# Seven-product 1024-column panels and ScalarE convolution taps in the channel mixers of a two-layer decoder trunk

## The chip, the cores and the metric

The kernel runs on one core of one Trainium2 chip. The metric is device time in microseconds (us) from the first to the last instruction of the program with what lies around it, as the median of several executions. The engines of the core have their own instruction queues: TensorE (PE, matmuls), with its weight loads shown apart as PEld; VectorE (DVE); ScalarE (ACT); GpSimd (POOL); SyncE (SP), which issues most of the DMAs. Matmul results land in PSUM, which has eight banks of 128 x 512 fp32.

## The reference, cut to what matters

There are 256 tokens, a model width of 2048 and two layers. Layer 0 mixes tokens by gated linear attention and layer 1 by forgetting attention; both also attend into 256 memory tokens. After each mixer comes a channel mixer, which is what the change touches:

```python
def causal_dwconv(u, w, b):
    up = jnp.pad(u, ((0, 0), (CONV_WIDTH - 1, 0), (0, 0)))
    return w[0] * up[:, 0:s_] + w[1] * up[:, 1:s_ + 1] + w[2] * up[:, 2:s_ + 2] + b

def conv_ffn(h, w_up, conv_w, conv_b, w_down):
    u = causal_dwconv(h @ w_up, conv_w, conv_b)
    a, val = split_cols(u, [FFN_HIDDEN, FFN_HIDDEN])
    return (jax.nn.silu(a) * val) @ w_down
```

The hidden width is 5632 (44 chunks of 128), so `w_up` is 2048 x 11264 and `w_down` is 5632 x 2048. Input to the mixer is `h = rmsnorm(x, norm_ffn)`, and its output is added to `x`. Everything is fp32.

## The kernel before

**Split products.** TensorE runs in the type fp32r. To keep fp32 accuracy each operand is held as a high part and a low part (the rest), and a product of two operands is three matmuls: high by high, low by high, high by low. The activations are the stationary operand (128 channels x 128 tokens); the weights are the moving operand (128 channels x up to 512 columns). There are two token blocks b of 128 tokens.

**Weight units.** Weights stream from HBM in units of 128 x 1024 fp32 (512 KB, tile `raw`, four buffers). ACT casts a unit to its high part `whi` (L207) and DVE subtracts that to get the low part `wlo` (L208), four buffers each. These instructions carry a priority of 300 places ahead of where they stand, so the planner puts them first as soon as a buffer is free. The planner (Tile's scheduler) lists the instructions of each engine in a fixed order by priority and by its own simulated times; the order on PE can therefore differ from that of the source.

**Panels.** An ordinary panel (`panel_tm`, matmuls at L310; `proj_tm`, matmuls at L282) has 512 output columns for both token blocks in two PSUM banks, and eight units of two channel chunks each: 8 x 2 x 2 x 3 = 96 matmuls for 16 chunks. The banks come from two pools: `acc` (four banks, tag acc) and the work banks (`ps_s` two, `ps_o` one, `ps_t` one).

**The channel mixer** (`ffn`, L1285) goes over the 44 hidden chunks in three parts (`PARTS`: 16, 16 and 12 chunks). In each part, up panels of two hidden chunks (256 columns of each half) come first. When an up panel is done, DVE transposes its two blocks out of PSUM by 32 x 32 squares (L611), a DMA writes them to DRAM (`far`) and four DMAs bring them back with channels on partitions (`close`). Then `convolve` works on one pair of hidden chunks: for each of the four 128 x 256 pieces DVE multiplies by the norm's row (L1306), ACT makes the last tap with scale and bias (L1310), DVE adds the other two taps (L1311, L1312); then ACT does silu (L1314), DVE multiplies the halves (L1315), and the result is split into high (L465) and low (L466) parts in the chunk buffers `m`. After the part's up panels the down panels of that part add to `x`. The first units of the down panels run while the last chunks of `m` are still being made.

**Pairs with seven products.** In parts 0 and 1, output columns 0 to 1023 are two ordinary panels, run nearly side by side. Output columns 1024 to 2047 are one panel over eight banks (`pair_tm`, L338): a chunk takes 12 matmuls (L377), but two chosen pairs of chunks (`SEVEN`) are handled as a 2 x 2 block product with seven products in place of eight (Winograd's form of Strassen's scheme): 21 matmuls (L363) in place of 24. For that DVE makes four sums of weight blocks (L393 to L396), which are split as well (L325, L326), and four sums of activations per pair (L1322 to L1325), and at the end combines p1, p5, p6 and p7 (L406 to L409). In part 2 all four down panels are ordinary.

**The norm.** The mixer's norm factor per token is applied after the up product, in `convolve`, as a row over tokens (`nx.row`), which costs a small matmul pair (L545).

## Time and profile before

| what | value |
|---|---|
| median of 3 runs | 2232.63 us (2232.56 to 2235.64) |
| the profiled execution, time | 2233.26 us |
| its span, first to last instruction | 2231.5 us |
| mean granted TensorE clock | 0.999 |
| PE busy | 2220.2 us (99%), 10405 matmuls |
| PEld busy | 1869.1 us (84%) |
| DVE busy | 1647.4 us (74%) |
| ACT busy | 1200.5 us (54%) |
| DMA queue of the weights | 510.66 MB, 73.2% of 16 engines |

The busy share of an engine says how full it is over the whole span, and the groups by line say what fills it. A mean of one instruction's duration is longer than the distance from its start to that of the next, when several follow each other without a gap; that distance, called pitch below, is read from a stretch of equal instructions in the timeline or in the chain. PE's durations overlap in this way above all. The chain of work that ended last tells which engine set the end at each moment.

### The profile page before, as it was taken

How to read it: one execution, taken by the hardware profiler on the slowest of the kernel's cores; microseconds unless marked ns; L12 is line 12 of the kernel's file. 1: busy time of each engine (PE TensorE's matmuls, PEld its weight loads, DVE VectorE, ACT ScalarE, POOL GpSimd, SP SyncE). 2: the span in 40 equal slices, each digit the busy share in tenths (PEclk: the TensorE clock that was granted, in tenths of full speed). 3: DMA queues.
4: the chain of work that ended last, by engine and by line, in shares of the span. 5: the costliest groups of instructions: out<-in, count | busy, mean ns of one | idle time of the engine just before them, and what ended most of it. 6: DMA issues, size and time to landing. Idle time of an engine off the chain costs nothing.

```text
span 2231.5 us, 29658 instructions
## 1 busy us (share of the span) xinstructions
PE 2220.2 (99%) x10405; PEld 1869.1 (84%) x10405; DVE 1647.4 (74%) x2754; ACT 1200.5 (54%) x1779; POOL 3.4 (0%) x19
## 2 busy tenths in 40 slices
PE   9999999999999999999999999999999999999998
PEld 7888888888888888888888998888888888888886
DVE  7768977668777687866777569666877677775776
ACT  6655664555554455545565455454655455553554
POOL 0000000000000000000000000000000000000000
PEclk9999999999999999999999999999999999999999
DMA  9777667777776777667787767778786678766774
GB/s 348 231 222 223 194 187 244 250 234 247 246 223 205 227 241 244 204 213 237 240 244 251 214 195 244 226 244 258 242 242 201 217 237 242 242 200 217 240 245 142
DMA packets 183053, 513.34 MB, mean 230 GB/s; under 512 B 20588, under 2 KB 66296, under 8 KB 182776
## 3 DMA queue, kind: packets, MB, share of 16 engines
q1 hardware_dynamic: 182328, 510.66, 73.2%
q8 instruction: 81, 1.33, 0.2%
q10 hardware_dynamic: 576, 0.79, 0.1%
q14 instruction: 68, 0.56, 0.1%
HBM read 468.63 MB, written 42.74 MB: 229 GB/s over the span
## 4 chain that ended last, share of the span: by engine, by line
PE 98%; DMA 1%; DVE 1%; ACT 0%; SPq 0%; issue 0%; DVEq 0%
PE acc L310 71%; PE ps_s L310 9%; PE acc L282 5%; PE ps_s L377 3%; PE acc L238 3%; PE ps_o L377 1%; PE ps_t L377 1%; PE acc L236 1%; PE acc L363 1%; PE ps_s L363 0%; PE ps_s L959 0%; DMA fky<-far 0%; DMA raw<-wp 0%; PE ps_o L635 0%; PE ps_s L635 0%; PE ps_o L363 0%
## 5 line engine op out<-in xcount | busy, mean ns | idle before, releaser
L208 DVE TENSOR_TENSOR wlo<-raw,whi 128x1024 fp32r<-128x1024 f32 (+4 forms) x793 | 948.2, 1198 | 502.5 <-ACT whi L207 483.4
L207 ACT ACTIVATE whi<-raw 128x1024 fp32r<-128x1024 f32 (+4 forms) x793 | 825.1, 1042 | 781.7 <-PE acc L310 504.2
L310 PE MATMUL acc<-whi,B 128*128 128x512 f32 (+3 forms) x2672 | 647.7, 380 | 0.0
L310 PEld LDWEIGHTS acc<-whi,B 128*128 128x128 f32 x2672 | 494.4, 188 | 83.5
L310 PE MATMUL acc<-whi,mix 128*128 128x512 f32 x1488 | 369.0, 389 | 0.0
L310 PE MATMUL acc<-wlo,B 128*128 128x512 f32 (+3 forms) x1336 | 352.7, 380 | 0.0
L310 PEld LDWEIGHTS acc<-whi,mix 128*128 128x128 f32 x1488 | 279.2, 188 | 57.9
L310 PEld LDWEIGHTS acc<-wlo,B 128*128 128x128 f32 x1336 | 248.2, 188 | 42.3
L310 PE MATMUL acc<-wlo,mix 128*128 128x512 f32 x744 | 200.4, 390 | 0.0
L310 PEld LDWEIGHTS acc<-wlo,mix 128*128 128x128 f32 x744 | 139.6, 188 | 28.9
L310 PE MATMUL acc<-whi,A 128*128 128x512 f32 x592 | 150.4, 389 | 0.0
L310 PEld LDWEIGHTS acc<-whi,A 128*128 128x128 f32 x592 | 111.1, 188 | 23.1
L1310 ACT ACTIVATE cv<-u,cw 128x256 f32<-128x256 f32 x176 | 95.1, 592 | 55.6 <-DVE u L1306 54.8
L310 PE MATMUL ps_s<-whi,mix 128*128 128x512 f32 x336 | 83.8, 389 | 0.0
L310 PE MATMUL acc<-wlo,A 128*128 128x512 f32 x296 | 83.6, 389 | 0.0
L1312 DVE SCALAR_TENSOR_TENSOR cv<-u,cw,cv 128x256 f32<-128x256 f32 x176 | 77.6, 478 | 0.0
L1311 DVE SCALAR_TENSOR_TENSOR cv<-u,cw,cv 128x256 f32<-128x256 f32 x176 | 76.0, 472 | 0.0
L310 PEld LDWEIGHTS ps_s<-whi,mix 128*128 128x128 f32 x336 | 63.0, 188 | 13.0
L310 PEld LDWEIGHTS acc<-wlo,A 128*128 128x128 f32 x296 | 55.4, 188 | 11.4
L1314 ACT ACTIVATE cv<-cv 128x256 f32<-128x256 f32 x88 | 36.7, 418 | 35.3 <-DVE cv L1312 31.7
L310 PE MATMUL ps_s<-whi,B 128*128 128x512 f32 x208 | 52.5, 389 | 0.0
L238 PE MATMUL acc<-mix,whi 128*128 128x512 f32 x192 | 48.9, 394 | 0.0
(346 smaller groups left out, 2062.8 us busy)
## 6 DMA issues: line engine op xcount, KB each, us to landing
raw<-wp SPq DMA_DIRECT2D x743, 512.0 KB, 4.3
fvt<-far SPq DMA_DIRECT2D x100, 128.0 KB, 5.8
raw<-wp SPq DMA_DIRECT2D x32, 384.0 KB, 3.4
yzu<-far SPq DMA_DIRECT2D x96, 128.0 KB, 5.7
far<-yu SPq DMA_DIRECT2D x22, 512.0 KB, 2.8
far<-yzu SPq DMA_DIRECT2D x22, 512.0 KB, 2.9
raw<-wp SPq DMA_DIRECT2D x24, 388.0 KB, 3.7
far<-blk SPq DMA_DIRECT2D x12, 512.0 KB, 3.4
```

The costliest lines, as they stand in the source:

```text
L207: casts.append(S.activation(hi[:, s], raw[:, s], AF.Copy))
L208: lows.append(V.tensor_tensor(lo[:, s], raw[:, s], hi[:, s].bitcast(F32), ALU.subtract))
L236: mm = TE.matmul(acc[p][c][:, :T], w[:, s], both[:, 0, :], start=False, stop=end and j == 3)
L238: mm = TE.matmul(acc[p][c], w[:, s], both, start=u == j == 0, stop=end and j == 3)
L282: mm = TE.matmul(acc[b][:, :n], src[kcs[j] - base][:, part, b * P : (b + 1) * P], w, start=u == 0 and low == part == j == 0, stop=u == end ...
L310: mm = TE.matmul(acc[b][:, :n], src[kc - base][:, part, b * P : (b + 1) * P], ready[low][:, j * n : (j + 1) * n], start=i == low == part = ...
L363: r = TE.matmul(bank[name], x[a], w[b], start=name not in begun, stop=last and i == 2)
L377: r = TE.matmul(bank[name], tok(k, b)[part], w[low][:, h * 512 : (h + 1) * 512], start=name not in begun, stop=last and low == 1)
L1310: S.activation(r, u[:, 2:], AF.Identity, bias=w[3], scale=w[2])
L1311: V.scalar_tensor_tensor(r, u[:, 1 : T + 1], w[1], r, ALU.mult, ALU.add)
L1312: V.scalar_tensor_tensor(r, u[:, :T], w[0], r, ALU.mult, ALU.add)
L1314: S.activation(cv[0], cv[0], AF.Silu)
```

## The change

It edits the channel mixers of both layers and what they use.

- Up panels: 20 of the 22 per layer are joined two by two into panels of 1024 columns (`WIDE`, ten per layer), which run through `pair_tm` with 16 units of one channel chunk each. One pair of input chunks (4 and 5, `SEVEN_UP`) goes by seven products in each; the sums of the inputs for it (`input_sums`) are made once per layer. Two ordinary up panels remain in part 2.
- Down panels: in parts 0 and 1 both halves of the output columns are now panels of 1024 columns with two pairs by seven products (`SEVEN_DOWN`, chunks 4 and 8 of the part); they run one after the other. In part 2 columns 0 to 1023 are one panel of 1024 columns without such pairs, and the two last panels stay ordinary.
- Banks: `pair_tm` uses four banks that live over the whole panel (p2, p3, p4, x) and four that live only from the first to the last seven-product pair (p1, p5, p7, p6). `flip` swaps from panel to panel which four come from `acc` and which from the work banks. `early` combines p1, p5, p6, p7 right behind the last such pair, `late` adds p2, p3, p4, x at the end. The weights of a pair are loaded into a tag of their own, `raw2`, with two buffers, and summed in place.
- The norm factor is applied per token block as a column (`nx.col`, a scale per partition) when an up panel is read from PSUM, so `nx.row` goes, and the transposes read SBUF instead of PSUM.
- `convolve`: for each piece ACT writes all three taps (one with scale and bias, two with a scale), 12 ACT instructions per call; DVE adds them in two instructions over 1024 elements; silu and the product of the halves are one instruction each over 512 elements.
- `close` is called at other places: at units 7 and 11 of the next up panel, at units 7 and 9 of the first down panel of parts 0 and 1, and at unit 4 of that of part 2.
- Room in SBUF: scratch tiles of the norms move to the pool of the stage, the final gain is loaded late into the input buffers, and the last panel's last three weight units are split by 512 columns into those buffers (`split_apart`).

```diff
--- before.py
+++ after.py
+WIDE = ((0, 4, 8, 12), (16, 20, 24, 28), (32, 36))
+SEVEN_UP = (4,)
+SEVEN_DOWN = (4, 8)
...
-                tm(("up", l, j), ("ffn_w_up", l), j * P, 2 * P, more=[(HID + j * P, 2 * P)])
+                if j in WIDE[p]:
+                    cols = [(c + (j + i) * P, 2 * P) for i in (0, 2) for c in (0, HID)]
+                    out.append((("up", l, j), ("ffn_w_up", l), full, cols, 1))
+                elif j - 2 not in WIDE[p]:
+                    tm(("up", l, j), ("ffn_w_up", l), j * P, 2 * P, more=[(HID + j * P, 2 * P)])
             last = p == len(PARTS) - 1
+            for f in (0, 2):
+                if f and last:
+                    break
+                out.append((("down", l, p, f), ("ffn_w_down", l), list(range(lo, hi)), [(f * 512, 1024)], 1))
+            for f in (2, 3) if last else ():
...
+        fast, slow = ("p1", "p5", "p7", "p6"), ("p2", "p3", "p4", "x")
+        accs, works = (slow, fast) if flip else (fast, slow)
+        tags = {n: ("acc", 4) for n in accs}
+        tags.update(zip(works, (("o", 1), ("s", 2), ("s", 2), ("t", 1))))
...
+            plan.append(k)
+            k += 2 if k in sums else 1
...
+        for k in plan:
+            if k in sums:
+                with tc.high_priority(offset=AHEAD):
+                    ra, rb = [pool.tile([P, NUNIT], F32, name="raw2", tag="raw2", bufs=2) for _ in range(2)]
+                    for t, (off, _, w) in ((ra, units[k]), (rb, units[k + 1])):
+                        loads.append(nc.sync.dma_start(t, wp[off : off + P * w].rearrange("(p n) -> p n", p=P)))
+                st = [[sums[k][:, part, j, :] for part in range(2)] for j in (3, 0, 1, 2)]
+                done = k == end[-1]
+                w1 = split_more(ra[:, :512], 512)
+                w2 = split_more(rb, 1024)
+                with tc.high_priority(offset=AHEAD):
+                    V.tensor_tensor(ra[:, :512], ra[:, 512:], ra[:, :512], ALU.subtract)
+                    V.tensor_tensor(ra[:, 512:], rb[:, 512:], ra[:, 512:], ALU.subtract)
+                    V.tensor_tensor(rb[:, 512:], rb[:, 512:], ra[:, :512], ALU.subtract)
+                    V.tensor_tensor(rb[:, :512], rb[:, :512], rb[:, 512:], ALU.subtract)
+                three("p1", tok(k, 0), [t[:, :512] for t in w1], done)
+                three("p2", tok(k + 1, 0), [t[:, :512] for t in w2])
+                three("p3", st[3], [t[:, 512:] for t in w2])
+                w3 = split_more(ra, 1024)
+                three("p5", st[0], [t[:, :512] for t in w3], done)
+                three("p7", st[2], [t[:, 512:] for t in w3], done)
+                w4 = split_more(rb, 1024)
+                three("p6", st[1], [t[:, 512:] for t in w4], done)
+                last_mm.append(three("p4", tok(k + 1, 1), [t[:, :512] for t in w4]))
+                if done:
+                    early(bank)
+                hooks.get(k + 1, int)()
+            else:
                 w = split_unit(units[k])
                 last = k == n - 1
+                steps = [(low, *place) for low in range(2) for place in places]
...
+                for low, name, b, h in steps:
+                    for part in range(2 - low):
+                        r = mm(name, tok(k, b)[part], w[low][:, h * 512 : (h + 1) * 512], last and low == 1)
+                    if last and low:
+                        ends.append(r)
+                        late(b, h, bank[name])
                 last_mm.append(r)
+            hooks.get(k, int)()
+    def token_sums(r, dst):
+        t = r.rearrange("p s (b n) -> p (s b) n", b=2)
+        a11, a21, a12, a22 = (t[:, n, :] for n in range(4))
+        V.tensor_tensor(a22, a21, a22, ALU.add)
+        V.tensor_tensor(a21, a11, a21, ALU.subtract)
+        V.tensor_tensor(a11, a22, a11, ALU.subtract)
+        V.tensor_tensor(a12, a12, a11, ALU.subtract)
+        halves([dst[:, part] for part in range(2)], t)
...
+    def down_pair(l, p, f, src, sums, flip, pool, temps, then=None, hooks={}):
+        def early(bank):
+            t0, t1 = temps()
+            S.activation(t0, bank["p1"], AF.Copy)
+            add_to(f)(0, t0)
+            V.tensor_tensor(t0, bank["p6"], t0, ALU.add)
+            V.tensor_tensor(t1, bank["p7"], t0, ALU.add)
+            add_to(f)(1, t1)
+            add_to(f + 1)(1, t1)
+            add_to(f + 1)(1, bank["p5"])
+            V.tensor_tensor(t0, bank["p5"], t0, ALU.add)
+            add_to(f + 1)(0, t0)
+        def late(b, h, a):
+            add_to(f + h)(b, a)
+            if then is not None:
+                then(f + h, b)
+        pair_tm(where["down", l, p, f], src, sums, flip, pool, early, late, hooks)
...
                         col = (c * 44 + j + s) * 4
                         w = [cw[:, col + n : col + n + 1] for n in range(4)]
+                        src = z[:, :, 2 * c + s]
+                        S.activation(by_run(taps[0][:, s, c, :]), src, AF.Identity, bias=w[3], scale=w[2])
+                        S.activation(by_run(taps[1][:, s, c, 1:]), src, AF.Copy, scale=w[1])
+                        S.activation(by_run(taps[2][:, s, c, 2:]), src, AF.Copy, scale=w[0])
+                t = taps[0]
+                for i_ in (1, 2):
+                    V.tensor_tensor(t, t, taps[i_][:, :, :, :T], ALU.add)
+                S.activation(t[:, :, 0, :], t[:, :, 0, :], AF.Silu)
+                r = fp.tile([P, 2, T], F32, name="cv", tag="cv")
+                V.tensor_tensor(r, t[:, :, 0, :], t[:, :, 1, :], ALU.mult)
+                for s in range(2):
+                    split(m, i + s, r[:, s, :])
...
+            def input_sums(k):
+                r = fp.tile([P, 2, T], F32, name="cv", tag="cv")
+                for s in range(2):
+                    V.tensor_tensor(r[:, s, :], h[k + s][:, 0, :].bitcast(F32), h[k + s][:, 1, :].bitcast(F32), ALU.add)
+                up_sums[k] = held("usum", k)
+                token_sums(r, up_sums[k])
...
+            def turn(j, i):
 
                 count[0] += 1
-                return panel_tm(("up", l, j), h, done, second)
+                y = ys[count[0] % 2]
+                def evac(b, a):
+                    with tc.high_priority(offset=AHEAD):
+                        V.transpose(y[:, :, :, b, :], a.rearrange("p (k c i) -> p c k i", c=4, i=32))
+                    if b:
+                        back = far_away(dram, flat(y), T)
+                        open_.append((j, i, back))
+                return evac
+            def up_pair(j, i, hooks):
+                count[2] += 1
+                turns = [turn(j + 2 * h_, i + 2 * h_) for h_ in range(2)]
+                u = {}
+                def early(bank):
+                    u.update({(b, h_): temps(2 * b + h_) for b in range(2) for h_ in range(2)})
+                    S.activation(u[0, 1], bank["p1"], AF.Copy)
+                    S.activation(u[0, 0], bank["p1"], AF.Copy, scale=scale(0))
+                    V.tensor_tensor(u[0, 1], bank["p6"], u[0, 1], ALU.add)
+                    V.tensor_tensor(u[1, 0], bank["p7"], u[0, 1], ALU.add)
+                    V.tensor_tensor(u[0, 1], bank["p5"], u[0, 1], ALU.add)
+                    V.tensor_tensor(u[1, 1], bank["p5"], u[1, 0], ALU.add)
+                    for b, h_ in ((0, 1), (1, 0), (1, 1)):
+                        S.activation(u[b, h_], u[b, h_], AF.Copy, scale=scale(b))
+                def late(b, h_, a):
+                    V.scalar_tensor_tensor(u[b, h_], a, scale(b), u[b, h_], ALU.mult, ALU.add)
+                    turns[h_](b, u[b, h_])
+                pair_tm(where["up", l, j], h, up_sums, count[2] % 2, pool, early, late, hooks)
...
+            def closing(*at):
+                return {k: lambda left=len(at) - 1 - i: close(left) for i, k in enumerate(at)}
...
+                for j in WIDE[p]:
+                    hooks = closing(7, 11)
+                    if p == 0 and j == lo:
+                        for k in SEVEN_UP:
+                            input_sums(k)
+                        hooks = {2: lambda: nx.land(landing[0]), 3: nx.take, 8: nx.col,
+                                 9: lambda: nx.land(landing[1]), 11: nx.take}
+                    up_pair(j, j - lo, hooks)
+                for j in range(lo, hi, 2):
+                    if j in WIDE[p] or j - 2 in WIDE[p]:
                         continue
                     step = up(j, j - lo)
                     for u in range(8):
                         step(u)
+                        if u in (2, 5):
+                            close(max(1, len(open_) - 1))
                 end = p == len(PARTS) - 1
+                for f in (0,) if end else (0, 2):
+                    hooks = {4: lambda: close(0)} if end else closing(7, 9) if f == 0 else {}
+                    if end:
+                        hooks[6] = getattr(then, "begin", int)
+                    count[2] += 1
+                    down_pair(l, p, f, m, {} if end else sums, count[2] % 2, pool, lambda: (temps(0), temps(1)),
+                              then if end else None, hooks)
+                sums.clear()
+            add_out(("down", l, len(PARTS) - 1), m, then=then, first=2, spare=spare, last=last)
...
```

244 lines of the change are left out of this document (86 added, 158 removed).

## The prediction

> **What bounds the kernel now.** I read the page's first and fourth parts, then the waits of PE, then the chain in order of time, then the stages by windows.
>
> ```profile
> span 2231.5 us, 29658 instructions
> PE 2220.2 (99%) x10405; PEld 1869.1 (84%) x10405; DVE 1647.4 (74%) x2754; ACT 1200.5 (54%) x1779; POOL 3.4 (0%) x19
> ...
> PE 98%; DMA 1%; DVE 1%; ACT 0%; SPq 0%; issue 0%; DVEq 0%
> ```
> ```profile
> PE ps_o L182 <- DVE B L179: 1.4, 1, 1.4
> PE ps_t L545 <- DVE dg L543: 0.8, 1, 0.8
> PE acc L282 <- ACT whi L207: 0.2, 1, 0.2
> ```
> ```profile
> 651.25 19.04 PE ps_s L310 x84
> 718.12 193.12 PE acc L310 x852
> ```
>
> The chain is PE nearly throughout, and all of PE's waits together are 2.4 us. So the time is a count of matmuls times their pitch, 193.12 / 852 = 0.2267 us: fewer matmuls pay in full, and every us in which PE has to wait is added. Whether it has to wait depends on VectorE and ScalarE, which split every weight unit just ahead of PE. Here are three stages of layer 0: the last two panels of part 0 with seven products, the eight up panels of part 1, and its two ordinary down panels. The columns are length, then busy us and count of PE, PEld, DVE, ACT and POOL.
>
> ```profile
> 675.57:718.12 42.55, 42.55 (x188) 35.09 (x187) 31.43 (x35) 21.51 (x22) 0.00 (x0) 1.00 0.62 199
> 718.12:892.24 174.12, 174.12 (x770) 144.22 (x769) 125.78 (x193) 89.10 (x116) 0.00 (x0) 1.00 0.77 236
> 892.24:935.73 43.49, 43.49 (x193) 36.03 (x192) 34.52 (x55) 22.66 (x32) 0.00 (x0) 1.00 0.68 215
> ```
>
> In the up stage DVE is busy for 125.78 / 174.12 = 72% and ACT for 51%; in the seven-product stage DVE is at 74%. Both have slack everywhere. The change spends it.
>
> **Matmuls, step by step.** A panel of 16 chunks has 96 matmuls, two joined ones have 192, and a joined panel with one seven-product pair has 14 x 12 + 21 = 189. Ten per layer: 30 fewer. Down, parts 0 and 1: 96 + 96 + 186 becomes 186 + 186, 6 fewer per part, 12 per layer. Part 2 keeps 288. That is 42 per layer, 84 in all, x 0.2267 = **-19.0 us**. The Trainium skill, "TensorE: Matmul & The Clock Gate", section "Wait — 56ns, not 53.3ns?", has 215.7 ns from start to start for 512 columns; by that page it would be 18.1 us as an estimate, but the trace has 0.2267 us over 852 matmuls, and that decides.
>
> The norm's row goes: two small matmuls (0.23 us, below) in each layer, **-0.5**.
>
> ```profile
> 52.78 0.23 PE ps_t L545 x2
> ```
>
> Seven-product matmuls are a little slower. From 651.25 to 718.12 lie 84 + 24 + 186 = 294 matmuls, 66.64 us at the plain pitch, but 66.87 us passed: 0.23 for two pairs, 0.115 each. After the change there are 20 + 16 = 36 pairs in place of 8: 28 x 0.115 = **+3.2** (ends: 0 if that loss belongs to something else, 6.4 if all 0.23 comes with each pair).
>
> **What VectorE and ScalarE pay.** Prices of the operations, by shape:
>
> ```profile
> L208 DVE TENSOR_TENSOR wlo<-raw,whi 128x1024 fp32r<-128x1024 f32 x727 | 885.5, 1221 | 457.4 <-ACT whi L207 446.7 <-PE acc L282 4.4 <-PE acc L236 2.7
> L1312 DVE SCALAR_TENSOR_TENSOR cv<-u,cw,cv 128x256 f32<-128x256 f32 x176 | 77.6, 478 | 0.0
> L1306 DVE TENSOR_TENSOR u<-fvt,row 128x256 f32<-128x256 f32 x88 | 31.6, 419 | 0.0
> L611 DVE STREAM_TRANSPOSE yu<-acc 128x512 f32<-128x512 f32 x42 | 29.8, 710 | 1.9 <-PE acc L310 1.9
> L435 DVE TENSOR_TENSOR x<-x,acc 128x512 f32<-128x512 f32 x36 | 24.3, 681 | 3.4 <-PE acc L310 3.4
> L1402 DVE STREAM_TRANSPOSE blk<-x 128x512 f32<-128x512 f32 x24 | 17.0, 708 | 0.5
> L394 DVE TENSOR_TENSOR tsum<-raw 128x512 f32<-128x512 f32 x8 | 5.5, 690 | 3.5 <-DMA raw<-wp 3.5
> L207 ACT ACTIVATE whi<-raw 128x1024 fp32r<-128x1024 f32 x727 | 769.5, 1059 | 723.5 <-PE acc L310 450.5 <-PE ps_t L377 57.4 <-issue 56.6
> L1310 ACT ACTIVATE cv<-u,cw 128x256 f32<-128x256 f32 x176 | 95.1, 592 | 55.6 <-DVE u L1306 54.8 <-DVE tsum L1323 0.8
> L1314 ACT ACTIVATE cv<-cv 128x256 f32<-128x256 f32 x88 | 36.7, 418 | 35.3 <-DVE cv L1312 31.7
> L465 ACT ACTIVATE mix<-cv 128x256 fp32r<-128x256 f32 x60 | 21.7, 403 | 0.4 <-DVE cv L1315 0.4
> L476 ACT ACTIVATE mix<-fvt,gains 128x256 fp32r<-128x256 f32 x12 | 5.4, 496 | 0.0
> L325 ACT ACTIVATE whi<-raw 128x512 fp32r<-128x512 f32 x8 | 5.0, 625 | 6.6 <-PE ps_s L310 6.6
> ```
> ```profile
> 689.46 2.35 DVE L208 TENSOR_TENSOR wlo<-raw,whi 128x1024 fp32r<-128x1024 f32 x2
> ...
> 696.15 1.89 DVE L435 TENSOR_TENSOR x<-x,ev 128x512 f32<-128x512 f32 x3
> ...
> 1107.32 1.43 DVE L1306 TENSOR_TENSOR u<-fvt,row 128x256 f32<-128x256 f32 x4
> ...
> 1127.81 2.07 ACT L1310 ACTIVATE cv<-u,cw 128x256 f32<-128x256 f32 x4
> ...
> 2226.32 0.75 DVE L1480 SCALAR_TENSOR_TENSOR x<-x,root,gf 128x512 f32<-128x512 f32 x1
> ```
>
> Back to back they overlap: the second 1024-wide one adds 1.13, a 512-wide one 0.60, a 256-wide one 0.34, an ACT tap 0.49. These pitches are the fairer measure of what fits: for two up panels of before they give 16 x 1.13 + 4 x 0.65 + 2 x (8 x 0.34 + 8 x 0.40) = 32.5 of 43.5 us, 75%, against the 72% measured; with whole durations it would be 84%.
>
> One convolve call: DVE falls from 8 x 0.42 + 8 x 0.48 = 7.2 us to two adds, a product and two low parts, 2 x 1.22 + 0.69 + 2 x 0.42 = 4.0 (pitch 3.5). ACT rises from 4 x 0.59 + 2 x 0.42 + 2 x 0.40 = 4.0 to 4 x 0.59 + 8 x 0.50 + 0.62 + 0.81 = 7.8. The tap with a scale alone is not in the trace in this place; L476 is the same form with the same runs of 32 (0.496), with 0.403 and 0.592 as ends.
>
> One joined up panel, 189 x 0.2267 = 42.8 us of PE. DVE: 14 low parts 17.1, the seven-product pair 0.69 + 3 x 1.22 + 4 x 0.69 = 7.1, `early` 4 x 0.69 = 2.8, `late` 4 x 0.75 = 3.0 (from PSUM it isn't in the trace: ends 0.68 of L435 and twice the 0.48 of L1312; nearest is L1480, of this kind and width), transposes 2.8, two convolves 7.9: 40.7 us, 95%; by pitch 37, 87%. ACT: casts 14.8, pair 3.8, five copies of 512 3.5 (0.625 for L325's width, 0.09 more with a scale, as L476 against L465), convolves 15.5: 37.6, 88%; by pitch 32, 76%. Both fit, so I put nothing on the up stages: what covers the new work is the slack counted above, and if it were gone DVE would be late next. The planner puts splits first, so PE waits only if the splits themselves are late, and they take 24 of 43 us.
>
> The first down panel of parts 0 and 1 doesn't fit. PE takes 186 x 0.2267 = 42.2 us; DVE by pitch has 12 low parts 13.6, two pairs 12.8, `late` and transposes of the up panel before 5.4, `early` 8 x 0.60 = 4.8, `late` 2.4 and the two last convolves 7.1: 46 us. The next down panel has 34, so most can slide into it, but the convolves can't: their chunks are due at units 12 and 14, 31.3 and 36.7 us after the start. Moved with `close` are its DMAs:
>
> ```profile
> raw<-wp SPq DMA_DIRECT2D x743, 512.0 KB, 4.3
> ...
> yzu<-far SPq DMA_DIRECT2D x96, 128.0 KB, 5.7
> far<-yu SPq DMA_DIRECT2D x22, 512.0 KB, 2.8
> ```
>
> The first block is transposed about 4 us into the panel, lies in DRAM at 7 and is back at 14 (four issues, 5.7 to land). SP issues in order, so behind it stand the weights of the second pair, which wait for the two `raw2` buffers anyway (about 12), and the second return, landing near 20. ACT fits the 12 taps between casts until about 25, DVE adds, ACT does silu, DVE multiplies and splits: about 32, 1 us late. For the second, DVE has 9 low parts 10.2, the two pairs 12.8, the up panel's `late` and transposes 5.4, `early` 4.8, the first convolve 3.5 and its own adds and product 2.9: 39.6 us in the 37.4 us that it has until unit 14, and 1.3 us of silu and split behind: 3 us late. Part of this PE bridges with the next panel's units; it does so now:
>
> ```profile
> 1135.71 1.98 PE L282 MATMUL acc<-whi,mix 128*128 128x512 f32 x8
> ...
> 1140.24 0.62 PE L310 MATMUL acc<-whi,mix 128*128 128x512 f32 x2
> ```
> ```profile
> 1127.27 1.43 DVE L1306 TENSOR_TENSOR u<-fvt,row 128x256 f32<-128x256 f32 x4
> ...
> 1137.29 0.75 DVE L466 TENSOR_TENSOR mix<-cv,mix 128x256 fp32r<-128x256 f32 x2
> ```
>
> There PE takes units of the third down panel (L282) before the last units of the first (L310), while the last convolve runs from 1127 to 1138. Four buffers limit this to what lies within four units; after unit 12 two of them serve the next panel. I take 1.5 us per place, two parts in two layers: **+6.0** (ends 0, all bridged, and 20, nothing bridged and DVE idle while the second pair's weights land). In part 2 without pairs DVE has room for both convolves: nothing.
>
> Bank handover: joined panels alternate, and `early` frees four banks some 27 us ahead of their next use, so 0; only the first one of a layer follows an ordinary panel whose last bank is still being added to `x` (0.68): **+0.5** for both. The late load of the final gain lies behind weight loads with six units, 16 us, of cover, and the 512-wide splits of the last panel cost 0.2 us of ACT per unit beside idle time: 0. The end, 8.8 us behind the last matmul at 2222.71, stays.
>
> ```profile
> 2195.21 27.50 PE acc L282 x120
> ```
>
> **Sum:** -19.0 - 0.5 + 3.2 + 6.0 + 0.5 = -9.8 us. The profiled execution took 2233.26 us (span 2231.5), so 2223.5; the median shown, 2232.63, lies 0.6 below it, so **2223**.
>
> **Rivals.**
>
> *The down panels give all of it back.* If the four places cost 4 us each and nothing is bridged, the sum is +0.2 and the time 2233 (2228 to 2237). For it: 46 us of DVE work against 42. Against it: the bridging above.
>
> *Slower: VectorE becomes the bound of the up panels.* It has 2.1 us of room per panel by durations, 5.7 by pitch. Its queue is in order, and the adds of a convolve now wait for 12 ACT instructions; a low part behind such an add waits too. If waits of this kind pass the room by 1 us in each of 20 panels, 20 us are added: 2243. It decides from 0.5 us over the room on. Against it: L208 now idles 457 us in all, mostly behind casts that themselves wait for PE.
>
> *Slower: a stalled PE restarts slowly.* The only matmuls of this trace that follow an idle PE are the first nine:
>
> ```profile
> L182 PE MATMUL ps_o<-B x9: 628/628/792, 1.4 to 5.0; 128*128 128x512 f32 x9
> ```
>
> Their starts are (5.0 - 1.4) / 8 = 0.45 us apart, so nine cost 2.0 us more than at 0.2267. If each of the four places stalls 5 us and then loses 2.0, 28 us replace the 6.0: 2245. The Trainium skill, "TensorE: Matmul & The Clock Gate", section "Part 1: The HAM clock gate (the "warmup" mystery)", says that the clock falls to half after an idle window of about 3.4 us; by that rule a shorter wait costs only itself. No row shows such a wait inside the run, as PE never idles there.
>
> **How the numbers follow.** Chances: forecast 0.67 (own range 2213, where every added cost is 0, to 2228), all given back 0.13, VectorE bound 0.13, slow restarts 0.07. A measurement can tell about 0.2%, 4.5 us, from no change, so faster (below 2228) 0.67, same 0.13, slower (above 2237) 0.20. The range of 2213 to 2240 leaves out the upper part of the last two and a little below.
>
> **What would show it.** 10405 - 84 - 4 = 10317 matmuls; joined up panels 42.8 us apart in the chain; DVE near 80% of the span (1647.4 - 44 x 3.2 + 28 more pairs x 4.7 + 20 x 5.8 + 4 x 5.5 = 1776) and ACT near 67% (1200.5 + 44 x 3.8 + 28 x 1.7 + 20 x 3.5 = 1485). PE's list of waits should name the chunks of `m` in the first down panels of parts 0 and 1, with 0 to 5 us each, and nothing in the up stages. The prediction is wrong if PE waits for `wlo` in up panels (VectorE bound), if matmuls of more than 0.45 us follow a wait (restarts), or if the pitch in joined panels is above 0.23 throughout.

## The result: 5% slower

The changed kernel takes 2346.59 us (median of 4, 2343.56 to 2348.26), the kernel before, beside it, 2233.06 us: a ratio of 1.0504, 95% interval 1.0486 to 1.0523. That is 113.5 us more, with 88 matmuls fewer.

The page of the profiled execution, its first part (busy time):

```profile
span 2344.3 us, 29896 instructions
PE 2247.9 (96%) x10317; PEld 1869.6 (80%) x10317; DVE 1790.5 (76%) x2639; ACT 1425.3 (61%) x2258; POOL 3.3 (0%) x15
```

The matmuls are gone as forecast and no engine beside PE is near full. But PE is no longer busy throughout. Its waits (engine, tile, line, what it waited for: us in all, times, longest) were 2.4 us before. Now the list begins so, and adds up to 87 us:

```profile
PE ps_t L373 <- ACT whi L349: 23.8, 8, 5.8
PE ps_s L373 <- ACT whi L349: 23.6, 6, 6.4
PE ps_o L373 <- ACT whi L230: 14.5, 8, 2.5
PE acc L373 <- ACT whi L230: 12.0, 6, 3.1
```

PE waits for ScalarE's casts of weights, `whi`: L230 for ordinary units, L349 for the pairs with seven products. By place, the waits of 0.3 us and more are 47 us in the four first down panels, 29 us in the joined up panels and 9 us in part 2's down panels. ScalarE is busy only 61% of the span, so the question is what it does just then. Its own waits name it:

```profile
ACT tap L1347 <- DMA yzu<-far: 15.5, 7, 5.4
ACT tap L1347 <- DMA fvt<-far: 15.2, 7, 4.7
ACT tap L1348 <- DMA fvt<-far: 15.1, 8, 4.0
ACT tap L1348 <- DMA yzu<-far: 14.4, 6, 4.5
```

For 60 us ScalarE stands at a convolution tap whose input, the block on its way back from DRAM, has not landed. The timeline of the first down panel of layer 0 (start, us, engine, line, operation, in brackets the idle time before and what ended it) shows what that does:

```profile
653.94 0.69 DVE L400 TENSOR_TENSOR raw<-raw 128x512 f32<-128x512 f32 x1
...
655.93 0.60 ACT L1347 ACTIVATE tap<-fvt,cw 128x256 f32<-128x256 f32 x1 [2.00 <-DMA fvt<-far]
...
659.81 0.59 ACT L1347 ACTIVATE tap<-fvt,cw 128x256 f32<-128x256 f32 x1
660.30 1.04 ACT L349 ACTIVATE whi<-raw 128x1024 fp32r<-128x1024 f32 x1
...
661.40 1.22 PE L373 MATMUL ps_t<-whi,dsum 128*128 128x512 f32 x2 [4.85 <-ACT whi L349]
662.42 3.35 PE L373 MATMUL acc<-whi,mix 128*128 128x512 f32 x8
...
667.39 1.06 ACT L349 ACTIVATE whi<-raw 128x1024 fp32r<-128x1024 f32 x1 [2.82 <-DMA raw<-wp]
667.46 1.98 PE L373 MATMUL acc<-whi,mix 128*128 128x512 f32 x8
...
672.77 0.52 ACT L1348 ACTIVATE tap<-fvt,cw 128x256 f32<-128x256 f32 x1 [3.80 <-DMA fvt<-far]
...
677.08 2.08 PE L373 MATMUL ps_s<-whi,dsum 128*128 128x512 f32 x4 [4.66 <-ACT whi L349]
```

ScalarE waits 2.00 us for a returned block, does ten taps in a run (655.93 to 660.30), and only then the cast, whose input (the weight sum at L400) had been there since 654.63; PE has waited 4.85 us for that. It happens again at 672. Behind the wait, eight matmuls take 3.35 us, which at 667.46 take 1.98. The stages by windows (length, PE busy us and count, granted clock, DMA share, GB/s) say why:

```profile
656.00:658.00 2.00, 0.55 (x2) 1.00 0.59 182
658.00:660.00 2.00, 0.00 (x0) 0.62 0.21 84
660.00:662.00 2.00, 0.60 (x2) 0.50 0.00 0
662.00:664.00 2.00, 2.00 (x6) 0.50 0.22 35
664.00:666.00 2.00, 2.00 (x7) 0.67 0.97 301
666.00:668.00 2.00, 2.00 (x11) 1.00 1.07 203
```

The granted clock falls to half during the wait and stays there until about 665. Over the whole span its mean is 0.981, against 0.999 before: 0.018 x 2344 = 42 us of full clock are missing, though part of that lies in the waits themselves. The Trainium skill, "TensorE: Matmul & The Clock Gate", section "Part 1: The HAM clock gate (the "warmup" mystery)", gives the two rates as half and full, and the trace agrees: 0.50 and 1.00.

### The profile page after: what moved, and what is told of

It reads as the page before. It is cut to its first block, busy times and chain, and to the rows that moved or that the text cites. A ratio compares the mean times of both kernels' runs of the same rounds, so it can differ in the third digit from the quotient of the medians.

```text
span 2344.3 us, 29896 instructions
## 1 busy us (share of the span) xinstructions
PE 2247.9 (96%) x10317; PEld 1869.6 (80%) x10317; DVE 1790.5 (76%) x2639; ACT 1425.3 (61%) x2258; POOL 3.3 (0%) x15
## 5 line engine op out<-in xcount | busy, mean ns | idle before, releaser
L231 DVE TENSOR_TENSOR wlo<-raw,whi 128x1024 fp32r<-128x1024 f32 (+4 forms) x734 | 868.5, 1197 | 343.6 <-ACT whi L230 326.2
L230 ACT ACTIVATE whi<-raw 128x1024 fp32r<-128x1024 f32 (+4 forms) x734 | 751.5, 1039 | 491.2 <-PE acc L334 184.8
L334 PE MATMUL acc<-whi,B 128*128 128x512 f32 (+3 forms) x1376 | 323.9, 371 | 0.0
L334 PEld LDWEIGHTS acc<-whi,B 128*128 128x128 f32 x1376 | 251.1, 188 | 33.1
L349 ACT ACTIVATE whi<-raw 128x1024 fp32r<-128x1024 f32 (+1 forms) x144 | 137.2, 953 | 198.4 <-DVE raw L398 62.4
L350 DVE TENSOR_TENSOR wlo<-raw,whi 128x1024 fp32r<-128x1024 f32 (+1 forms) x144 | 155.7, 1082 | 77.1 <-ACT whi L349 73.7
L373 PEld LDWEIGHTS acc<-whi,mix 128*128 128x128 f32 x850 | 168.9, 200 | 49.3 <-ACT whi L230 10.2
L373 PE MATMUL acc<-whi,B 128*128 128x512 f32 x730 | 191.1, 394 | 8.6 <-ACT whi L230 3.7
L334 PE MATMUL acc<-wlo,B 128*128 128x512 f32 (+3 forms) x688 | 176.0, 371 | 0.0
L373 PEld LDWEIGHTS acc<-whi,B 128*128 128x128 f32 x730 | 138.5, 190 | 39.7 <-ACT whi L230 4.8
L334 PEld LDWEIGHTS acc<-wlo,B 128*128 128x128 f32 x688 | 126.6, 188 | 16.9
L1352 DVE TENSOR_TENSOR tap<-tap,tap 128x1024 f32<-128x1024 f32 x88 | 107.4, 1221 | 18.7 <-ACT tap L1348 12.8
L373 PE MATMUL acc<-wlo,B 128*128 128x512 f32 x365 | 105.1, 393 | 0.1
```

The source lines that it names most:

```text
L230: casts.append(S.activation(hi[:, s], raw[:, s], AF.Copy))
L231: lows.append(V.tensor_tensor(lo[:, s], raw[:, s], hi[:, s].bitcast(F32), ALU.subtract))
L334: mm = TE.matmul(acc[b][:, :n], src[kc - base][:, part, b * P : (b + 1) * P], ready[low][:, j * n : (j + 1) * n], start=i == low == part = ...
L349: casts.append(S.activation(hi[:, :n], src, AF.Copy))
L350: lows.append(V.tensor_tensor(lo[:, :n], src, hi[:, :n].bitcast(F32), ALU.subtract))
L373: r = TE.matmul(bank[name], x, w, start=name not in begun, stop=last)
```

## The experiments

To compare kernels with different numbers of matmuls, "lost" below is the time, less that of the kernel before beside it, plus 0.2267 us for each matmul below 10405. The changed kernel has lost 113.5 + 88 x 0.2267 = 133.5 us, where the prediction had 9.7.

| kernel | matmuls | us | lost |
|---|---|---|---|
| changed kernel | 10317 | 2346.6 | 133.5 |
| e1: taps held behind the newest cast | 10317 | 2298.3 | 84.8 |
| e5: e1, blocks fetched earlier | 10317 | 2293.8 | 80.4 |
| e2: taps back on VectorE | 10317 | 2267.8 | 54.3 |
| e6: e2, three buffers for the second pair's weights | 10317 | 2267.5 | 54.1 |
| e8: e2, other places | 10317 | 2268.7 | 55.3 |
| e3: changed kernel, no pairs with seven products | 10425 | 2298.8 | 60.8 |
| e4: kernel before, taps on ScalarE | 10405 | 2237.3 | 3.9 |
| e7: e2, pairs only in up panels | 10365 | 2238.9 | 14.6 |
| e9: e7, pair at unit 6 | 10365 | 2235.3 | 11.3 |
| e10: e9, pairs also in the second down panels | 10341 | 2234.2 | 15.7 |
| e11: e7, two pairs in each up panel | 10305 | 2321.2 | 110.8 |
| e12: e9, taps on ScalarE behind the newest cast | 10365 | 2309.9 | 85.9 |
| e13: e12, taps in four groups | 10365 | 2276.8 | 52.7 |
| e14: e10, part 2's convolutions earlier | 10341 | 2224.9 | 6.2 |

The changed kernel, e9, e10 and e14 are medians of 4, 10, 10 and 7 runs; the others are single runs. The ten runs of e9 lie between 2231.68 and 2240.29 us, so a difference of a few us to a single run shows nothing by itself.

**The taps in ScalarE's queue.** In the kernel before, the first instruction of a convolution was DVE's multiply, and `close` holds that behind the newest low part; ScalarE's tap then came when the multiply was done. In the changed kernel the first instructions are ScalarE's taps, and the same tie, which works on the engine it names, doesn't hold them. e1 holds them:

```diff
+                        with tc.issue_after(casts[-1].ins):
                             S.activation(by_run(taps[0][:, s, c, :]), src, AF.Identity, bias=w[3], scale=w[2])
                             S.activation(by_run(taps[1][:, s, c, 1:]), src, AF.Copy, scale=w[1])
                             S.activation(by_run(taps[2][:, s, c, 2:]), src, AF.Copy, scale=w[0])
```

> The changed kernel with one edit: the twelve taps of a convolve may not stand ahead of the newest weight cast in ScalarE's queue (in the changed kernel only the VectorE part of convolve is held back like this). Theory A: taps stand in front of weight casts in ScalarE's in-order queue and wait there for the return DMA, PE waits for the cast, and restarts slowly. It expects 2235 to 2270 us in place of 2346.6, PE's waits down from 87 us to 25 or less. Theory B (VectorE has more work than fits into the down panels, and the weights of the second pair land late in two buffers) and theory C (a pair by seven products needs four splits in 4.8 us, more than four buffers can hide, whatever convolve does) expect no change, 2335 to 2350.

e2 puts two of the three taps back on VectorE and leaves the panels as they are:

```diff
-                        S.activation(by_run(taps[0][:, s, c, :]), src, AF.Identity, bias=w[3], scale=w[2])
-                        S.activation(by_run(taps[1][:, s, c, 1:]), src, AF.Copy, scale=w[1])
-                        S.activation(by_run(taps[2][:, s, c, 2:]), src, AF.Copy, scale=w[0])
+                        u, r = taps[2][:, s, c, :], taps[0][:, s, c, :]
+                        V.tensor_copy(by_run(u[:, 2:]), src)
+                        S.activation(r, u[:, 2:], AF.Identity, bias=w[3], scale=w[2])
+                        V.scalar_tensor_tensor(r, u[:, 1 : T + 1], w[1], r, ALU.mult, ALU.add)
+                        V.scalar_tensor_tensor(r, u[:, :T], w[0], r, ALU.mult, ALU.add)
```

> The changed kernel with its taps back on VectorE: a copy of each piece, one tap on ScalarE behind it, two on VectorE, all behind the newest low part; panels, pairs and banks as changed. Theory A: nothing on ScalarE waits for the return DMA any more, 2240 to 2275 us, with no ScalarE wait for that DMA. Theory B: VectorE gets some 4 us more work per call, two calls per 42.8 us, and is far beyond what fits: 2370 or more. Theory C: 2340 to 2350.

e3 takes the seven products out of the changed kernel (`SEVEN_UP = SEVEN_DOWN = ()`; its joined up panels are read from PSUM by ScalarE, with the scale, where the changed kernel has VectorE do it), and e4 goes the other way and gives the kernel before the taps on ScalarE, each behind DVE's multiply:

> The changed kernel with no pair by seven products at all (panels of 1024 columns, taps on ScalarE and the closing places stay; the up panels are read from PSUM by ScalarE with the scale). 108 matmuls more than changed, 24 more than before. Theory A: the taps still block the casts: 2270 to 2330 us, PE waiting for casts in the up panels. Theories B and C: PE is never late, 2233 + 24 x 0.227 = 2238, within 5 us.

```diff
-                        V.scalar_tensor_tensor(r, u[:, 1 : T + 1], w[1], r, ALU.mult, ALU.add)
-                        V.scalar_tensor_tensor(r, u[:, :T], w[0], r, ALU.mult, ALU.add)
+                        for n in range(2):
+                            S.activation(t12[n], u[:, 1 - n : T + 1 - n], AF.Copy, scale=w[1 - n])
+                            V.tensor_tensor(r, r, t12[n], ALU.add)
```

> The kernel before with the other part of the change alone: all three taps on ScalarE, two adds on VectorE; VectorE still multiplies by the norm's row first, so no ScalarE instruction reads the returned block itself (cv tiles with two buffers in place of three to make room). Theory A: ScalarE has room (54% busy) and its taps follow VectorE's multiply, so the same time as before, 2228 to 2240 us. If the taps on ScalarE cost by their work alone: 2260 or more.

Measured: e1 2298.28, e2 2267.81, e3 2298.81, e4 2237.29 us. VectorE's work is more in e2 than in the changed kernel (82% busy against 76%), and yet it is 78.8 us faster: VectorE was not what the changed kernel lacked. e4 has 128 us more of ScalarE work than the kernel before and costs 3.9 us: the taps' work alone isn't it either, in that kernel's panels of 512 columns. e3, without any pair, still loses 60.8 us (PE's waits there are 42 us, 9.3 of them for ScalarE's reading of the ordinary up panels out of PSUM at L1419) and shows the longest waits of taps for returned blocks:

```profile
ACT tap L1347 <- DMA yzu<-far: 78.3, 11, 8.2
ACT tap L1347 <- DMA fvt<-far: 67.3, 11, 7.4
```

So place in the queue is the cause of the larger part: 48.3 us (e1) go by holding the taps behind a cast, 78.8 (e2) by taking them off ScalarE. e2, e3 and e4 lie in theory A's ranges. e1 lies outside both of its own, nearer to A's, with 48 us of waits of PE where A had 25 or less, and that left 30.5 us between e1 and e2. e5 asked whether those are late blocks, by issuing the return transfers two or three units earlier on top of e1 (`hooks.update({k: fetch for k in (2, 3)})`):

> The kernel after with two edits: the taps are held behind the newest cast of a high part (as in e1_tie, 2298.3 us), and the transfers that bring the pieces back are issued two or three units earlier than the taps that read them. Theory A (the taps stand ahead of the casts in ScalarE's in-order queue and wait there, above all for the return transfer): the tie has already taken that wait down to 4.0 us, so earlier transfers bring little more: 2285 to 2300, and ScalarE's waits of taps on the return transfer below 5 us. Rival D (what is left in e1_tie, 97 us over the full pitch, is still the lateness of the returned pieces, now borne by VectorE's adds): 2250 to 2275.

2293.82 us, 4.5 less than e1: no. (The waits of taps for blocks were 6.7 us, a little above the 5 expected.) What the rest is, e12 and e13 ask on a kernel without pairs in the down panels, where e9 is the partner with the taps on VectorE. In e13 `convolve` hands out its twelve taps by threes, one unit of 12 matmuls apart, and the down panels also close their convolutions at other units:

```diff
                             S.activation(by_run(taps[2][:, s, c, 2:]), src, AF.Copy, scale=w[0])
+                        yield
...
-                        convolve(j, i, z, j < PARTS[-1][0] and i in SEVEN_DOWN)
+                        if next(now[0], 1):
+                            now.clear()
...
-                return {k: lambda left=len(at) - 1 - i: close(left) for i, k in enumerate(at)}
+                hooks = {k + n: more for k in at for n in range(1, 5)}
...
-                    hooks = {4: lambda: close(0)} if end else closing(7, 9) if f == 0 else {}
+                    hooks = closing(1, 5) if end else closing(5, 9) if f == 0 else {}
```

> As e9_up_six, with the taps of after on ScalarE, held behind the newest cast as in e1_tie. e1_tie was 30 us slower than e2_taps_dve, which has the taps on VectorE. If the taps on ScalarE cost this only together with the pairs in the down panels (ScalarE's queue full with the casts of two pairs): 2229 to 2238. If ten taps in a row delay the casts of any panel in which a convolution stands: 2245 to 2262.

> As e12_up_taps (2309.9 us: one pair of seven products in the up panels, at unit 6, eight products in all down panels, the taps on ScalarE, each held behind the newest cast at its place in the program), with the twelve taps of a convolution handed out in four groups of three, one unit of 12 matmuls apart, in place of all at one place. Theory A2 (the cost is that the twelve taps run in one stretch of 4.4 us ahead of the cast that TensorE needs next): at most three taps, 1.2 us, stand ahead of any cast, and most of the 75 us over e9_up_six (2235.3 us) goes: 2236 to 2262. Rival I (ScalarE has no room for the taps wherever they stand, since casts and taps together come late): 2290 to 2320.

e12 took 2309.88 us, 74.6 more than e9, far above what was expected of the tie. ScalarE's timeline in an up panel of e12, tie and all:

```profile
566.98 0.60 ACT L1348 ACTIVATE tap<-fvt,cw 128x256 f32<-128x256 f32 x1 [2.44 <-DMA fvt<-far]
...
570.86 0.59 ACT L1348 ACTIVATE tap<-fvt,cw 128x256 f32<-128x256 f32 x1
571.35 1.04 ACT L230 ACTIVATE whi<-raw 128x1024 fp32r<-128x1024 f32 x1
```

The same convolution in e13:

```profile
567.81 1.04 ACT L230 ACTIVATE whi<-raw 128x1024 fp32r<-128x1024 f32 x1
568.76 0.59 ACT L1348 ACTIVATE tap<-fvt,cw 128x256 f32<-128x256 f32 x1
...
570.05 1.05 ACT L230 ACTIVATE whi<-raw 128x1024 fp32r<-128x1024 f32 x1
```

And in the kernel before, where each tap waits for its own multiply and a cast slips in between:

```profile
566.08 0.60 ACT L1310 ACTIVATE cv<-u,cw 128x256 f32<-128x256 f32 x1 [1.63 <-DVE u L1306]
566.58 1.04 ACT L207 ACTIVATE whi<-raw 128x1024 fp32r<-128x1024 f32 x1
567.53 1.58 ACT L1310 ACTIVATE cv<-u,cw 128x256 f32<-128x256 f32 x3
569.01 1.05 ACT L207 ACTIVATE whi<-raw 128x1024 fp32r<-128x1024 f32 x1
```

In e12 ten taps, 4.4 us, follow the tied cast, and the next cast stands behind them; a tie to the cast before says nothing about the cast after. In e13 the same convolution has six taps ahead of the first cast and three and two between the next ones, and 33.1 of the 74.6 us go. PE's waits of e12, then of e13:

```profile
PE ps_o L373 <- ACT whi L230: 17.8, 11, 2.6
PE acc L373 <- ACT whi L230: 11.3, 5, 3.5
PE acc L373 <- ACT B L484: 11.2, 4, 4.2
```

```profile
PE acc L373 <- ACT B L484: 11.1, 4, 3.8
PE acc L373 <- ACT whi L230: 7.9, 7, 2.3
PE acc L373 <- ACT mix L484: 6.8, 2, 4.2
```

The waits for casts of ordinary units shrink from 29.1 us (two rows) to 7.9. In the joined up panels, whose closing places e13 leaves alone, they go from 28.6 to 1.8 us. There the run of ten taps, with the wait at its head, was what cost. ScalarE's taps wait 26.2 us for returned blocks in e12 and 14.0 in e13, and the two runs don't separate the length of the run from that wait. What doesn't shrink are the waits for the chunks of `m` made last (L484): with the smaller rows of the same kind 20.2 us in e12 and 22.1 in e13, against 5.6 in e9. So neither expectation holds in full. Rival I is refuted, since the same taps on the same engine, placed otherwise, cost 33 us less; but e13 lies above A2's 2236 to 2262, and in its down panels the convolutions with their taps on ScalarE still end too late. Whether a better spread would mend that too, or the chain through two engines is too long there, stays open, and with it 41.5 us between e13 and e9.

**The pairs in the down panels.** With the taps off ScalarE, e2 still loses 54.3 us. e6 gives the second pair's weights a third buffer, e7 takes the pairs out of the down panels (`SEVEN_DOWN = ()`), e8 moves the up panels' pair (`SEVEN_UP = (6,)`) and part 2's convolutions (units 1 and 3).

> As e2_taps_dve (2267.8 us), with three buffers in place of two for the second pair's weights (the tile of one tap, unused there, makes the room). Theory E (the stalls that are left in the first down panels, 34 us over the full pitch in e2_taps_dve, are the second pair's weights, which come late since their buffer comes free only when VectorE has summed the pair before): 2240 to 2258, and ScalarE's cast no longer waits for the load of a second pair. Rival F (they are VectorE's and ScalarE's work itself, with the nearly double number of casts and weight sums that two pairs in a panel bring): 2262 to 2270.

> As e2_taps_dve (2267.8 us), but the down panels keep the eight products: only the 36 up panels have a pair with seven, 10365 matmuls in place of 10317. If the stalls of the first down panels belong to the pairs with seven products there (weights loaded late, sums on VectorE, more casts), they go, 34 us, and 48 matmuls of 0.2267 us come back, 10.9 us: 2240 to 2250. If they belong to panels of 1024 columns and their convolutions in any case, they stay and the 48 matmuls are added: 2272 to 2282.

(The 36 in this text is a slip: 20 panels have such a pair; 40 matmuls is the net difference to the kernel before.)

> As e2_taps_dve (2267.8 us), with the pair of seven products of the up panels at unit 6 in place of 4, and in part 2 the two last convolutions closed at units 1 and 3 in place of both at unit 4. If the stalls of the first up panel of each layer (3.2 and 5.1 us over the full pitch in e2_taps_dve) and of part 2 (2.8 and 5.7) come from where this work stands in the order, they shrink: 2252 to 2264. If they come from the handover of the banks, they stay: 2266 to 2270. The first down panels are untouched by this edit and their 34 us should stay in both.

e6 took 2267.50 us: ScalarE's casts of such pairs wait less for the load (28.6 us in e2, 16.9 in e6), and the time stays. So the late weights, which the prediction had seen, are not what bounds these panels as far as this edit brings them earlier; it doesn't bring all of them. e7 took 2238.91 us, 1 us below the range: with the taps on VectorE the pairs in the down panels are worth 54.3 - 14.6 = 39.7 us of loss, against 10.9 us that their 48 matmuls save. The two causes don't add up as if they were apart: with the taps tied on ScalarE the kernel without these pairs (e12, 85.9) loses no less than the one with them (e1, 84.8). e8, at 2268.71, gained nothing: its first up panels no longer stall, but its first down panels wait longer (PE's `ps_s` for L349: 18.1 us for 6.7 in e2). e9 adds that place to e7, and e10 gives pairs back to the second down panels alone (`sums if f == 2 else {}`), in which no convolution is closed:

> As e7_up_only (2238.9 us: taps back on VectorE, pairs with seven products in the up panels alone, one in each of 20 panels, 10365 matmuls), with that pair at unit 6 in place of 4. In e8_places this edit took the stalls of the first up panel of each layer away (3.0 and 5.0 us over the full pitch in e7_up_only), and e8's growth in the first down panels needs the pairs there, which are gone. If places and pairs act apart like that: 2229 to 2234, at or just below the kernel before. If the stalls only move (as they did in e8_places, 2268.7 us for 2267.8): 2237 to 2242.

> As e9_up_six, with the two pairs of seven products in the second down panel of parts 0 and 1 only: the first one, in which the last two convolutions of the part are closed, keeps eight products. 10341 matmuls, 24 fewer than e9_up_six, 5.4 us. Theory G (the pairs stall only where they meet the convolutions' work in the same panel): no stalls in either, 2224 to 2230. Rival H (two pairs in a down panel are too much for VectorE and the weight loads in any panel, 8 to 11 us at each of four places): 2255 to 2272.

e9 took 2235.29 us, between its two ranges (ratio to the kernel before 1.0007, 0.9997 to 1.0016), e10 2234.21 us (1.0000, 0.9991 to 1.0010). e10's list of PE's waits holds no cast of a pair any more:

```profile
PE acc L373 <- ACT mix L484: 3.8, 2, 2.0
PE ps_t L564 <- DVE dg L562: 2.6, 1, 2.6
PE acc L373 <- ACT B L484: 2.5, 2, 1.9
```

The two pairs of a down panel stall, then, in the first panel, where they meet the last convolutions of a part, and not in the second: what theory G says. The first panel also takes in `late` and the transposes of the last up panel, and no run separates these from the convolutions. G's number missed, 2234 for 2224 to 2230: of the 5.4 us that 24 matmuls save 1.1 came, while PE's waits are 10.6 us in e10 and 7.5 in e9. e11 asks for more pairs where convolutions run, two in each up panel (`SEVEN_UP = (4, 8)`). In the first panel of a layer this kernel forms the second pair's sums before their input is taken in, so that part of its products is of older data; the instructions and their number are those of the full computation.

> As e7_up_only (2238.9 us), with two pairs of seven products in each up panel, at units 4 and 8: 60 matmuls fewer (10305), 13.6 us at full pace. If an up panel has room for a second pair: 2224 to 2230. If two pairs in one panel with convolutions stall it as they did the first down panels (some 8 us at each of four places), up panels do so at twenty places, 2 to 8 us each: 2265 to 2385.

2321.17 us, 82 more than e7. The casts of the pairs wait for loads and sums of weights (28.6 and 43.2 us in e2):

```profile
ACT whi L349 <- DMA raw<-wp: 80.0, 21, 6.3
ACT whi L349 <- DVE raw L398: 78.4, 35, 5.4
```

**A version that beats both.** What PE waits for in e10 are mostly the mixed chunks of part 2 (L484). e14 closes part 2's last convolutions earlier, and is otherwise e10. Against the changed kernel, beside the edit of e2:

```diff
-SEVEN_UP = (4,)
+SEVEN_UP = (6,)
...
-                    hooks = {4: lambda: close(0)} if end else closing(7, 9) if f == 0 else {}
+                    hooks = {1: lambda: close(1), 3: lambda: close(0)} if end else closing(7, 9) if f == 0 else {}
...
-                    down_pair(l, p, f, m, {} if end else sums, count[2] % 2, pool, lambda: (temps(0), temps(1)),
+                    down_pair(l, p, f, m, sums if f == 2 else {}, count[2] % 2, pool, lambda: (temps(0), temps(1)),
```

> As e10_second_down (2234.2 us), with the last two convolutions of part 2 closed at units 1 and 3 of its down panel in place of both at unit 4. In e10_second_down TensorE waits there for the mixed pieces, 4.5 and 5.1 us over the full pitch at two places. If they come earlier, 4 to 8 us go: 2226 to 2231, below the kernel before. If VectorE has no room for them there: 2232 to 2236.

2224.88 us (2222.03 to 2228.90), 1 us below the range; ratio to the kernel before 0.9964, 0.9953 to 0.9976, so 0.4% faster. Its page and its first waits:

```profile
PE 2208.8 (99%) x10341; PEld 1856.3 (84%) x10341; DVE 1804.1 (81%) x2999; ACT 1271.0 (57%) x1886; POOL 3.3 (0%) x15
```

```profile
PE ps_o L188 <- DVE B L185: 1.4, 1, 1.4
PE acc L373 <- ACT B L484: 1.2, 1, 1.2
```

This is the panel part of the change, without the pairs in the first down panels and with other places for the up panels' pair and part 2's convolutions, and with the taps left on the engines they had (a copy stands in for the multiply). It keeps 64 of the 88 matmuls and gains 8.3 us, with VectorE at 81%.

## Why the prediction was wrong

It forecast 2223 us and 9.7 us of added cost; 133.5 us came.

- **What bounds the kernel, and the matmuls.** The count is right: 10317. That each of them pays in full no run shows: e14, which hardly waits, got 8.3 of the 64 x 0.2267 = 14.5 us that its own count gives. The added 3.2 us for the slower seven-product matmuls could not be measured alone; in e14, with 20 more pairs, that term, 2.0 us of added waits and everything else come to 6.2.
- **The prices.** Right for VectorE: 1790.5 us busy against 1776 forecast. ScalarE was forecast too high, 1485 against 1425.3: a tap was priced at 0.50 us, and the 352 that e2 doesn't have add 135.9 us, 0.39 each (ten in a run take 4.4 us). So ScalarE had more room than the budget gave it, and the time was lost all the same.
- **"Both fit, so I put nothing on the up stages", "The planner puts splits first, so PE waits only if the splits themselves are late" and, for the first down panels, "ACT fits the 12 taps between casts".** This is the step that failed. The budget counted busy time per panel; it didn't ask in which order the planner lists ScalarE's work. Ten taps without a DVE instruction ahead of them went into the queue in one run, some of them before their input had landed, and a cast behind a waiting tap waits too. Of the 133.5 us lost, 79.2 go when the taps leave ScalarE (e2), and the up stages, where nothing was forecast, hold 29 us of PE's waits. PE waits for `whi` 80 us of its 87, at L230 in ordinary units and at L349 in the pairs.
- **+6.0 for the first down panels.** The place came true, the size and the mechanism didn't. These four panels hold 47 us of waits, all for high and low parts of the pairs' weights (L349, L350) and none for the chunks of `m` that the prediction named, so the right place is in part luck. The prediction let only the last chunks be late, and let the rest "slide into" the next panel. But the casts of the pairs' weight sums are due inside this panel; in the changed kernel the taps stood ahead of them, and with the taps on VectorE the pairs in the down panels still lose 39.7 us (e7 against e2). That the first panel with its convolutions is the place, e10 shows; which of VectorE's instructions is the one too many wasn't tried. (The prediction's 37.4 us until unit 14 doesn't fit the 36.7 that it gives just before; that moves its 3 us by 0.7.)
- **Part 2: "nothing", and +0.5 for the first panels.** Both too small: PE waits 9 us in part 2's down panels, and 9.5 us lie between e10 and e14; at the first up panel of the two layers PE's waits are 3.8 us in e7 and gone in e9.
- **The rival "VectorE becomes the bound".** The trace doesn't show it: PE's waits for low parts, VectorE's work, are 2.1 of the 87 us. In-order queues were the right thing to look at, but the prediction looked at VectorE's adds behind ScalarE, and the cost came from ScalarE's casts behind its own taps.
- **The rival "a stalled PE restarts slowly".** It came true, beside the failed step and not alone: 1.98 us became 3.35 for eight matmuls, and the two right behind the wait start 0.51 us apart, above the 0.45 that was named as its sign. By the clock records of the trace the clock was at half for 81.9 us, with PE busy in 63.9 of them, so about 32 us of pace were lost. Of the 133.5 us, then, 85 are waits (87.2 less the 2.4 of before) and 32 are pace; some 17 are left for waits too short for the list and for slower pairs. The rule that the prediction set beside this rival, that a shorter wait costs only itself, doesn't hold here, as the last section shows.

## What to carry to other kernels

A share of busy time says whether work fits, not whether it stands in front of something that is due. When an operation moves to another engine, look for what held it in place on the old one (here a multiply that came first and was tied to the weights) and write the new tie for the engine that now begins. A tie to an earlier cast does not protect the next one: hand such work out in small pieces. In e13, with three taps at a time, PE's waits for casts in the up panels went from 28.6 to 1.8 us.

## What the hardware showed unexpectedly

How long PE may wait before its clock falls isn't one number. In the changed kernel PE waited 1.97 us before 807.10 and went on at full clock; in e12 it waited 2.02 us before 524.05, and the clock fell to half after PE was back at work. The clock records of the traces show a pattern behind this. Every change of the clock in a trace lies on one grid of 3.413 us, which runs through the whole trace; cut at that grid, the windows are these (the changed kernel, then e12):

```profile
801.86:805.27 3.41, 3.28 (x15) 1.00 0.63 245
805.27:808.69 3.42, 1.59 (x7) 1.00 0.00 0
808.69:812.10 3.41, 3.41 (x17) 1.00 0.79 226
```

```profile
518.41:521.83 3.42, 3.42 (x16) 1.00 0.87 260
521.83:525.24 3.41, 1.39 (x6) 1.00 0.02 8
525.24:528.65 3.41, 3.41 (x10) 0.50 0.33 97
528.65:532.07 3.42, 3.42 (x16) 1.00 0.79 284
```

PE was idle for 1.83 us of the second window in the changed kernel and for 2.02 us in e12; behind the latter the next window has half the clock. In the traces of the 16 kernels here all 82 falls follow a window with 1.59 us or more of idleness, and none of the 10369 windows at full clock without a fall behind them has more than 1.88 us. So what counts, as far as these traces go, is whether PE idles for about half of one such window, in one wait or several, and a wait that straddles two windows may be free of it. The Trainium skill, "TensorE: Matmul & The Clock Gate", section "Part 1: The HAM clock gate (the "warmup" mystery)", has the clock fall after an idle window of about 3.4 us. The length of the window agrees; a whole window of idleness wasn't needed here, and the measurement decides: a wait of 2 us can cost the pace of the matmuls behind it.
